# Rotating images by 180 degrees: all loads from one queue, the first group in four stepped transfers

## The chip, the cores and the metric

The kernel runs on one core of a Trainium2 chip. The metric is the device time of one execution in microseconds; of the kernel before, three runs took 122.02, 122.11 and 122.21, median 122.11.

## The reference

The input is 32 x 3 images of 256 x 256 float32 numbers. Each image is turned by 180 degrees:

```python
def reference(x: np.ndarray) -> np.ndarray:
    return np.rot90(x, k=2, axes=(-2, -1)).astype(np.float32)
```

Seen as a flat list of 65,536 numbers, an image is simply reversed. Nothing is computed; 25.17 MB are read, and 25.17 MB are written.

## The kernel before

The 96 images form three groups of 32 (G = 32, L37 to L40). Within a group, each image is cut into four sections of E = 16,384 numbers (64 KB). Partition p = 4n + s of a tile holds section s of image n, so a group fills 128 partitions of 64 KB each. Three such tiles, `A`, `Bt` and `Ct`, hold the three groups at the same time; a fourth, `T`, has room for J = 2048 numbers per partition and serves as scratch.

A group passes three steps. `load` (L54, L55) brings it in with one DMA of 128 rows. `turn` (L73) reverses every partition's 16,384 numbers in place: it calls `swap` (L61) for a strip of at most 2048 columns at the left and its mirror strip at the right, and each swap is three VectorE copies (all recorded at L52): right strip reversed to T, left strip reversed to the right, T to the left. `store` (L57, L58) writes the tile back; the order of the four sections within an image is reversed by the access pattern on the DRAM side (`[:, ::-1, ...]`), which walks 32 images of 4 sections.

The order of the work is written out by hand. The loads stand first (L69 to L71): A and Ct are issued by SyncE (SP), Bt by ScalarE (ACT), which does nothing else. The loads of A and Ct share SP's DMA queue with all the stores, and that queue serves transfers in the order of issue; Bt's load has ACT's queue for itself. VectorE's copies are kept in program order: three of A's four strips (`turn(A, 0, half - J)`, L80), a strip of 1008 columns of Bt (MID, L82), the last strip of A (L83), the rest of Bt (L85), all of Ct (L87). A's store is split: columns 0 to 255 (LEAD, L81), which are final after the first swap, and the other 16,128 columns (L84). The stores of Bt and Ct (L86, L88) are whole. SP issues a store when VectorE has finished the strips that it holds.

Of the kernel before, what the change touches and what calls it, by code (L numbers as in the profile page):

```python
# [2 lines left out]

os.environ.setdefault("NEURON_RT_ULTRASERVER_MODE", "4")

# [4 lines left out]


@with_exitstack
def kernel(
    ctx: ExitStack,
    tc: tile.TileContext,
    x: bass.AP,
    out: bass.AP,
):

    nc = tc.nc
    P = 128

    B, C, H, W = x.shape
    L = H * W
    G = 32
    E = L // 4
    J = E // 8

    x4 = x.rearrange("b c h w -> (b c) (h w)").rearrange(  # L37
        "(g n) (s e) -> g (n s) e", n=G, s=4)
    o4 = out.rearrange("b c h w -> (b c) (h w)").rearrange(
        "(g n) (s e) -> g n s e", n=G, s=4)  # L40

    pool = ctx.enter_context(tc.tile_pool(name="slots", bufs=1))
    A = pool.tile([P, E], x.dtype, tag="A")
    Bt = pool.tile([P, E], x.dtype, tag="B")
    Ct = pool.tile([P, E], x.dtype, tag="C")
    T = pool.tile([P, J], x.dtype, tag="T")

    def back(t, lo, hi):
        return t[:, hi - 1:(lo - 1 if lo else None):-1]

    def copy(dst, src):
        tc.keep_in_program_order(nc.vector.tensor_copy(out=dst, in_=src))  # L52

    def load(t, g, lo, hi, queue=nc.sync):  # L54
        return queue.dma_start(out=t[:, lo:hi], in_=x4[g][:, lo:hi])  # L55

    def store(t, g, lo, hi):  # L57
        return nc.sync.dma_start(  # L58
            out=o4[g][:, ::-1, lo:hi], in_=t[:, lo:hi])

    def swap(t, lo, w):  # L61
        hi = E - lo - w
        copy(T[:, 0:w], back(t, hi, hi + w))
        copy(t[:, hi:hi + w], back(t, lo, lo + w))
        copy(t[:, lo:lo + w], T[:, 0:w])

    MID = 1008
    LEAD = 256
    load(A, 0, 0, E)  # L69
    load(Bt, 1, 0, E, nc.scalar)  # L70
    load(Ct, 2, 0, E)  # L71

    def turn(t, lo, hi):  # L73
        while lo < hi:
            w = min(J, hi - lo)
            swap(t, lo, w)
            lo += w

    half = E // 2
    turn(A, 0, half - J)  # L80
    store(A, 0, 0, LEAD)  # L81
    turn(Bt, 0, MID)  # L82
    turn(A, half - J, half)  # L83
    store(A, 0, LEAD, E)  # L84
    turn(Bt, MID, half)  # L85
    store(Bt, 1, 0, E)  # L86
    turn(Ct, 0, half)  # L87
    store(Ct, 2, 0, E)  # L88


# [1 line left out]
_INS = ['x']  # L92
_OUTS = [((32, 3, 256, 256), 'float32')]


# [23 lines left out]
```

## Time and profile before

| what | value |
|---|---|
| median of three runs | 122.11 us |
| span of the profiled execution, first to last instruction | 120.5 us (its time outside the span isn't listed; the median is 1.6 us above the span) |
| VectorE busy | 44.7 us, 39 copies; one of 128 x 2048 takes 1.23 us |
| load of A (SP) and of Bt (ACT), issued at 0.73, to landing | 41.2 and 41.4 us |
| load of Ct (SP), issued at 1.18, to landing | 60.5 us |
| first copy of VectorE | at 41.99 us |
| stores issued to landing: A small, A large, Bt, Ct | 16.3, 21.9, 27.6, 31.8 us |
| DMA traffic | 50.33 MB, mean 418 GB/s over the span |

A DMA is shared out over the core's 16 DMA engines. The trace records each packet of each engine; here a packet is one row of one partition (64 KB, or 1 KB in A's small store), and every transfer ends on each engine with a packet of 4 bytes that raises a semaphore. "Issue" is the instruction on SP or ACT that hands the transfer over; "landing" is the moment when its last semaphore update has arrived. Queue 1 is SP's, queue 10 is ACT's.

The profile's stretches give for each window the busy time of the engines, the granted clock, the mean busy share of the DMA engines and the bytes moved. The list of waits says who waited for whom, and how long.

### The profile page before, as it was taken

To read this page: it belongs to the slowest core of one execution; us is meant where nothing else is said; L and a number is where in the kernel's file an instruction comes from. 1 tells how busy PE (TensorE), PEld (TensorE's weight loads), DVE (VectorE), ACT (ScalarE), POOL (GpSimd) and SP (SyncE) were. 2 spreads that over 40 slices of the span, in tenths; PEclk is the share of its full clock that TensorE was granted. 3 is DMA by queue.
4 is the path that set the end of the run, shared out by engine and by line. 5 is a ranking of instruction groups with operands and counts; after the bars stand their busy time and mean duration, and the time that the engine had idled before them with its cause. 6 is when DMAs were issued, how large, how long until landed. Compare 5 with 4: busy or idle time off the path is not lost.

```text
span 120.5 us, 96 instructions
## 1 busy us (share of the span) xinstructions
DVE 44.7 (37%) x39; POOL 0.2 (0%) x4
## 2 busy tenths in 40 slices
DVE  0000000000000099999999999999910000000000
POOL 0000000000000000000000000000000000000000
DMA  9888988898889888988999977988898889888980
GB/s 348 348 348 370 674 348 348 370 652 370 348 370 652 370 348 348 674 370 348 348 386 599 428 343 343 664 369 348 348 674 370 348 348 674 370 348 348 674 370 0
DMA packets 1008, 50.33 MB, mean 418 GB/s; under 512 B 112, under 2 KB 240, under 8 KB 240
## 3 DMA queue, kind: packets, MB, share of 16 engines
q1 hardware_dynamic: 864, 41.94, 81.3%
q10 hardware_dynamic: 144, 8.39, 16.1%
HBM read 25.17 MB, written 25.17 MB: 418 GB/s over the span
## 4 chain that ended last, share of the span: by engine, by line
DVE 37%; DMA 34%; issue 1%
DMA A<-in_x_dram 34%; DVE T L52 12%; DVE Bt L52 9%; DVE A L52 8%; DVE Ct L52 8%
## 5 line engine op out<-in xcount | busy, mean ns | idle before, releaser
L52 DVE COPY T<-A 128x2048 f32<-128x2048 f32 x4 | 4.9, 1227 | 42.1 <-DMA A<-in_x_dram 42.0
L52 DVE COPY Bt<-T 128x2048 f32<-128x2048 f32 (+2 forms) x5 | 5.1, 1014 | 0.2
L52 DVE COPY T<-Bt 128x2048 f32<-128x2048 f32 (+2 forms) x5 | 5.1, 1014 | 0.2
L52 DVE COPY Bt<-Bt 128x2048 f32<-128x2048 f32 (+2 forms) x5 | 5.1, 1013 | 0.2
L52 DVE COPY T<-Ct 128x2048 f32<-128x2048 f32 x4 | 4.9, 1228 | 0.1
L52 DVE COPY A<-T 128x2048 f32<-128x2048 f32 x4 | 4.9, 1227 | 0.1
L52 DVE COPY Ct<-T 128x2048 f32<-128x2048 f32 x4 | 4.9, 1227 | 0.1
L52 DVE COPY Ct<-Ct 128x2048 f32<-128x2048 f32 x4 | 4.9, 1227 | 0.1
L52 DVE COPY A<-A 128x2048 f32<-128x2048 f32 x4 | 4.9, 1226 | 0.1
L103 POOL MEMSET const-bfloat16-1.0<- 128x1 bf16 x1 | 0.1, 101 | 0.0
L103 POOL MEMSET const-uint8-127<- 128x1 uint8 x1 | 0.1, 101 | 0.0
L103 POOL MEMSET const-float32-0.0<- 128x1 f32 x1 | 0.1, 98 | 0.2 <-issue 0.2
L103 POOL MEMSET const-float32-1.0<- 128x1 f32 x1 | 0.1, 98 | 0.0
## 6 DMA issues: line engine op xcount, KB each, us to landing
out_dram<-A SPq DMA_DIRECT2D x1, 8064.0 KB, 21.9
out_dram<-A SPq DMA_DIRECT2D x1, 128.0 KB, 16.3
Bt<-in_x_dram ACTq DMA_DIRECT2D x1, 41.4
A<-in_x_dram SPq DMA_DIRECT2D x1, 41.2
Ct<-in_x_dram SPq DMA_DIRECT2D x1, 60.5
out_dram<-Bt SPq DMA_DIRECT2D x1, 27.6
out_dram<-Ct SPq DMA_DIRECT2D x1, 31.8
```

The costliest lines, as they stand in the source:

```text
L52: tc.keep_in_program_order(nc.vector.tensor_copy(out=dst, in_=src))
L103: nc = _bacc.Bacc("TRN2", target_bir_lowering=False, num_devices=1)
```

## The change

ScalarE no longer issues a load. SyncE issues all of them: group 0 in four transfers of 32 rows, where transfer j brings section j of all 32 images to the partitions j, j + 4, j + 8, ...; then group 1 whole, then group 2 whole. The copies, the stores and their order stay. (Eight empty lines are also taken out, so that line numbers after the change are lower by 8 up to the loads.)

```diff
     MID = 1008
     LEAD = 256
-    load(A, 0, 0, E)
-    load(Bt, 1, 0, E, nc.scalar)
+    for j in range(4):
+        nc.sync.dma_start(out=A[j::4, :], in_=x4[0][j::4, :])
+    load(Bt, 1, 0, E)
     load(Ct, 2, 0, E)
```

VectorE's first copy of A then waits for four semaphores in place of one, and so does A's small store. In the order of instructions, ACT loses its one DMA; SP has ten DMAs in place of six.

## The prediction

> **What bounds the kernel now.** I first read the page's top lines: VectorE, the only engine that computes, is busy 37% of the span, so it can't be the bound by itself. Then the lines of the DMA queues, and the busy time by stretches, cut where one transfer ends and the next begins (columns: stretch and its length, busy time of DVE and POOL, clock, mean busy share of the 16 DMA engines, GB/s):
>
> ```profile
> span 120.5 us, 96 instructions
> ...
> DVE 44.7 (37%) x39; POOL 0.2 (0%) x4
> ...
> q1 hardware_dynamic: 864, 41.94, 81.3%
> q10 hardware_dynamic: 144, 8.39, 16.1%
> ```
>
> ```profile
> ...
> 1.75:41.60 39.84, 0.00 (x0) 0.00 (x0) 1.00 1.04 446
> 41.60:61.20 19.60, 18.66 (x17) 0.00 (x0) 1.00 0.91 385
> 61.20:80.20 19.00, 18.45 (x17) 0.00 (x0) 1.00 1.00 434
> 80.20:99.50 19.30, 7.54 (x7) 0.00 (x0) 1.00 1.00 435
> 99.50:118.80 19.30, 0.00 (x0) 0.00 (x0) 1.00 1.00 435
> ```
>
> The two queues fill 81.3 + 16.1 = 97.4% of 16 engines' span. The transfers follow each other without a hole: A with Bt to 41.6, Ct to 61.2, then the stores of A, Bt, Ct at 434 to 435 GB/s. (A packet is booked at its end, which makes the first share 1.04 and the second 0.91.) The trace's packet records say how. A packet is one row of 64 KB; each engine moves 8 rows of each group. The first row takes 2.70 to 3.37 us (median 3.10), every other load row up to 44 us 2.418 to 2.44, every 64 KB store row 2.418, one beginning each 2.4145. Each engine has 48 such rows in a chain: 48 x 2.4145 = 115.9, the pieces of A's store counted as 8 whole rows. Beside them stand 0.7 for the first row, about 0.4 in the last Ct rows, 1.76 before the first packet and about 1.1 after the last, and the staggering of the engines. That is the 120.5.
>
> The list of waits names something else:
>
> ```profile
> DVE T L52 <- DMA A<-in_x_dram: 42.0, 1, 42.0
> ```
>
> VectorE stands still for 42.0 us until A has landed. The reader is to see that this wait is long and yet not the bound: the engines work all through it. The page's DMA issues (line, queue, count, KB, us from issue to landing) show the same for the stores:
>
> ```profile
> out_dram<-A SPq DMA_DIRECT2D x1, 8064.0 KB, 21.9
> out_dram<-A SPq DMA_DIRECT2D x1, 128.0 KB, 16.3
> ...
> out_dram<-Bt SPq DMA_DIRECT2D x1, 27.6
> out_dram<-Ct SPq DMA_DIRECT2D x1, 31.8
> ```
>
> 128 KB take 16.3 us to land because they stand behind Ct's load in SP's queue: issued at 45.77, their packets move at 60.93 and after. Ct's store, issued at 88.0, lands at 119.7: it needs 19.3 and waits 11 behind Bt's. The queue is served in the order of issue.
>
> **The change, part by part.**
>
> *A comes first, alone.* Before, A and Bt take turns row by row (queue 1, queue 10), so both land at 42. After, A's 8 rows per engine run first: the slowest engine ends its first row at 5.38, seven more make 5.38 + 7 x 2.4145 = 22.3, and with the 0.5 from the last packet to the landing (41.61 to 42.14 now) VectorE starts at about 22.8 in place of 41.99. Nine copies of A at a pitch of 1.26 end at 34.1. The next copies read Bt, which lands at 42 as before (the bytes ahead of it are the same), so VectorE stops for 8 us. Then 3 x 0.72 on Bt and 3 x 1.26 on A: the large store of A goes out at about 48.0 (59.3 now). Bt's remaining 13.6 end at 61.6 (72.8 now); Ct has landed at 61.7, its 15.1 end at 76.9 (88.0 now).
>
> *What that is worth: nothing.* The stores stand behind the loads in the queue and begin at 61 in either kernel. A's large store is needed there at about 61.3; its first packet would come 1.0 after issue (0.73 to 1.76 at the start), so it is 12 us early, where it is 1 early now. Bt's is needed at 80.2, Ct's at 99.5; both are ready long before, now too (72.8 and 88.0). The 19 us on VectorE and the 11 us on the issues become waiting in the queue. The stall that goes was never the late one; the queue is.
>
> *Bt moved from ACT's queue to SP's.* ACT issues nothing else and is released from its 0.38 of issue. On SP, Bt's issue moves behind four of A's and Ct's behind five, at 0.45 a piece (0.73 to 1.18 now): Bt at 2.5, Ct at 3.0. Engines have A's rows until 21, so neither is missed. Nothing else waits on SP: its next instruction is A's small store.
>
> *A in four transfers.* Three more issues and, per engine, three more 4-byte semaphore packets of 9 ns on the path: +0.03. The second quarter is issued at 1.2 and has packets at about 2.2; an engine asks for it after two rows, at about 7.2, so the cover is 5 us. Were the cover gone, an engine would idle by what is missing. Does the border of two transfers itself cost? In one queue the large store of A is followed by Bt's, Bt's by Ct's: the records show a 9 ns packet and the next row at once. Loads behind loads: A's end (41.0) to Ct's first row, the same, though queue 10 ended there too. I take 0; the upper end is a restart like the very first row's, 0.64 (the mean of the 16 first rows, 3.06, less 2.418) at each of four borders: 2.6.
>
> *The first row.* First packets leave from 1.755 to 2.483 over the engines, first rows end from 4.75 to 5.38. A first transfer with a quarter of the rows and no second issuer beside it may start the late engines sooner. If all ended as the earliest: -0.63. If the latest start met the longest excess (0.95): 2.48 + 2.42 + 0.95 = 5.85, +0.47. The late starters had the short excess (0.28 to 0.41), so start and end are loosely tied, and I take -0.1.
>
> *A store waiting longer in the queue.* Ct's rows are even until A's small store is issued at 45.8; the five rows that follow it show medians 5, 0, 27, 7, 26 ns over 2.418 (sum 0.07), and the last load row 0.35. If the queued store is the cause, the five become twelve rows (issued at 26.6): 12 x 0.013 = 0.16, +0.09; at 27 each +0.26. If not, 0 (or -0.07 were they to vanish). I take +0.05. The 0.35 belongs to the last load row ahead of the stores, which stays.
>
> *The end.* SP's last waits get three more semaphores, all long fired: 0.02 each, +0.05. VectorE's first copy and A's small store wait for four instead of one: off the path.
>
> Sum against the span: -0.1 + 0.03 + 0.05 + 0.05 = +0.03, so 120.5 again. The median of the runs, 122.11, is 1.6 above that span; the page doesn't split it, and nothing in the change touches it. 122.1.
>
> **A rule that speaks against it.** The Trainium skill (SBUF — State Buffer, "Can I just issue two DMAs to hit both halves?") says that only one transfer spanning all 128 partitions reaches all 16 ports, and its section on the setup-cost knee puts about 2 us of fixed cost on each transfer; three more would give 122.1 + 6 = 128 as an estimate by that page. The rows here show no such cost between queued transfers (9 ns), so the measured border is used. By the port map of the same page (Door 1), every fourth partition meets each port twice, so the first half of the rule need not bite if the rows are dealt to the engines by port; that dealing no row of before shows for 32 rows.
>
> **The rivals.**
>
> *Slower: the 32 rows are dealt unevenly.* All of the above needs two rows of each quarter on each engine, with no two engines in each other's way. If only 8 engines carry them (or two share one way into SBUF), A takes 16 row times instead of 8 on those: +8 x 2.4145 = 19.3, 141.4. It decides as soon as an engine gets three rows of each quarter (+9.7). Against it: the stores' DRAM side is walked as 32 x 4 rows (issue forms 32x4x16384), and they run at 2.418 a row on all 16. For it: no 32-row load with stepped partitions is in the trace.
>
> *Slower: borders cost.* Each of the four new borders on the single queue costs some part of a restart, because loads behind loads on one queue alone were never seen: +0.3 to +2.6, say 123.4. Against: the store borders.
>
> *Faster: the start shrinks and the slowest engine with it.* The end is set by the slowest engine (last packets end from 118.85 to 119.40), and its lag dates from the first row. At -0.4 for the start, 121.7; with a quiet queue as well 121.4. For it: the spread of 0.73 between engines at the start, with two issuers.
>
> **How the numbers follow.** About 0.2% (0.24 us) is what a measurement of this kernel can tell from no change. Forecast, within that: 0.44. Faster by the start: 0.28. Borders: 0.15. Uneven dealing: 0.13. So slower 0.28 in all. The range runs from 121.4 (the whole faster case but its end) to 123.4 (more than half of the borders): 0.44 + 0.27 + 0.09 = 0.80. The forecast's own range is 121.9 to 122.35.
>
> **What would show it.** Right: A's last quarter lands at about 22.5 and VectorE's first copy starts there, stops 8 us for Bt, the large store of A issues near 48, and yet Ct's store lands near 119.7. Queue 1 alone holds all 50 MB. Wrong: A landing at about 40 (uneven dealing); rows longer than 2.42 at the start of each quarter (borders); first rows all ending by 4.9 (the faster case); stores moving before 61 would overturn the order of the queue.

## The result and the profile after

The changed kernel is slower by about 1%: 123.25 us (median of 4 runs, 123.23 to 123.37) against 122.06 (4 runs, 121.82 to 122.21). The ratio over all runs is 1.0105, 95% interval 1.0091 to 1.0119 (the two medians alone give 1.0097). The profiled execution has a span of 121.6 us against 120.5.

The page of the changed kernel, lines that answer to those shown of before (its DMA issues: line, queue, count, KB, us from issue to landing):

```profile
span 121.6 us, 102 instructions
...
DVE 44.6 (37%) x39; POOL 0.2 (0%) x4
...
q1 hardware_dynamic: 1056, 50.33, 97.0%
...
out_dram<-A SPq DMA_DIRECT2D x1, 8064.0 KB, 33.8
out_dram<-A SPq DMA_DIRECT2D x1, 128.0 KB, 36.2
...
Ct<-in_x_dram SPq DMA_DIRECT2D x1, 58.8
out_dram<-Bt SPq DMA_DIRECT2D x1, 39.5
out_dram<-Ct SPq DMA_DIRECT2D x1, 42.8
```

One queue now holds all 50.33 MB, and the stores spend 11 to 20 us more between issue and landing: they wait in the queue. The list of waits of the changed kernel (who waited for whom, us, times, longest):

```profile
DVE T L44 <- DMA A<-in_x_dram: 23.1, 1, 23.1
DVE T L44 <- DMA Bt<-in_x_dram: 8.0, 1, 8.0
DVE T L44 <- DMA Ct<-in_x_dram: 0.9, 1, 0.9
```

VectorE starts at 23.1 instead of 42.0 and stops 8.0 for Bt, as worked out. The third line is new and small, and it is the trace of the loss: Ct lands at 62.7 (issued at 3.89, 58.8 to landing), 1.0 later than the 61.7 of before.

Where is that microsecond? Here are SP's and ACT's first issues in the timelines (start, duration, queue, line, what), of the changed kernel and then of before:

```profile
0.73 2.49 SPq L62 DMA_DIRECT2D A<-in_x_dram  x4
3.26 0.58 SPq L47 DMA_DIRECT2D Bt<-in_x_dram  x1
3.89 0.45 SPq L47 DMA_DIRECT2D Ct<-in_x_dram  x1
```

```profile
0.73 0.38 ACTq L55 DMA_DIRECT2D Bt<-in_x_dram  x1
0.73 0.39 SPq L55 DMA_DIRECT2D A<-in_x_dram  x1
1.18 0.43 SPq L55 DMA_DIRECT2D Ct<-in_x_dram  x1
```

A stepped quarter takes some 0.6 to issue (2.49 for four), a whole group 0.4 before; Bt's whole load right behind the quarters takes 0.58 as well. In the packet records the first packet leaves at 2.09 instead of 1.76, and the slowest engine ends its first row at 5.69 instead of 5.38: **+0.31**. This place varies from execution to execution: in the runs below that begin on a whole load (e1, e2, e4 to e7, e10, e11) the slowest first row ended at 5.25 to 5.57, in the other one that begins on a stepped quarter (e8) at 6.07. From there on the rows of A and Bt are 2.418 to 2.44 in both, also at the borders of the quarters.

The second place is the last row that each engine loads. The next two answers are the stretches around its end (stretch, length, busy DVE and POOL, clock, DMA share, GB/s; a packet is booked at its end, so a stretch in which no row ends shows 0). First the changed kernel, then before:

```profile
58.90:60.30 1.40, 1.36 (x2) 0.00 (x0) 1.00 0.00 0
60.30:61.50 1.20, 1.13 (x3) 0.00 (x0) 1.00 0.00 0
61.50:62.80 1.30, 0.40 (x2) 0.00 (x0) 1.00 2.13 895
```

```profile
58.90:60.30 1.40, 1.37 (x2) 0.00 (x0) 1.00 0.00 0
60.30:61.50 1.20, 1.17 (x2) 0.00 (x0) 1.00 1.78 744
61.50:62.80 1.30, 1.27 (x2) 0.00 (x0) 1.00 0.49 208
```

Before, the rows end in the middle stretch; after, in the last one. On the slowest engines the row before it ends at 58.60 and 58.84 (after), the last load row at 61.40 and 62.38: the lag grows there from 0.24 to 0.98, and 0.98 it stays until the last packet (119.40 and 120.38). (It had shrunk from 0.31 to 0.24 because five of Ct's rows were a little longer before, by 0.07 in sum.) A last load row takes 3.02 to 3.80 us, where an undisturbed one takes 2.42, and 2.73 to 2.80 in this profile of before. The end of the span adds 0.06.

### The profile page after: what moved, and what is told of

It reads as the page before. It is cut to its first block, busy times and chain, and to the rows that moved or that the text cites. A ratio compares the mean times of both kernels' runs of the same rounds, so it can differ in the third digit from the quotient of the medians.

```text
span 121.6 us, 102 instructions
## 1 busy us (share of the span) xinstructions
DVE 44.6 (37%) x39; POOL 0.2 (0%) x4
## 2 busy tenths in 40 slices
DMA packets 1056, 50.33 MB, mean 414 GB/s; under 512 B 160, under 2 KB 288, under 8 KB 288
## 3 DMA queue, kind: packets, MB, share of 16 engines
q1 hardware_dynamic: 1056, 50.33, 97.0%
## 4 chain that ended last, share of the span: by engine, by line
DMA 32%; DVE 28%; SPq 2%; issue 1%; another core or an unknown queue 1%; DVEq 0%
DMA Bt<-in_x_dram 32%; DVE T L44 9%; DVE Bt L44 8%; DVE Ct L44 8%; DVE A L44 2%; SPq L62 2%; DVEq L44 0%
## 5 line engine op out<-in xcount | busy, mean ns | idle before, releaser
L44 DVE COPY T<-A 128x2048 f32<-128x2048 f32 x4 | 4.9, 1227 | 23.2 <-DMA A<-in_x_dram 23.1
## 6 DMA issues: line engine op xcount, KB each, us to landing
Ct<-in_x_dram SPq DMA_DIRECT2D x1, 58.8
```

## The experiments

The theory after reading the two traces: A's stores, issued early because A lands early, stand in the queue behind the loads, and this lengthens the last load row (theory Q); the quarters cost only at the start. The rivals: the quarters do both, or the single queue does. "Row" below is the time of Ct's last load row over the 16 engines, from the packet records. Times are medians; the ratio is over all runs, to the kernel before on the same chip (its medians: 122.02 beside e1 to e4, 122.11 beside e5 to e8, 121.88 beside e9 to e11), and so not quite the quotient of the medians.

| run | edit | ratio (95%) | us | first packet | row, us |
|---|---|---|---|---|---|
| changed | quarters on SP, all loads on SP | 1.0105 (1.0091 to 1.0119) | 123.25 | 2.09 | 3.02 to 3.80 |
| e1 | three whole loads on SP | 1.0079 (1.0062 to 1.0096) | 123.13 | 1.74 | 2.95 to 3.77 |
| e2 | quarters on SP, Bt on ACT | 1.0008 (0.9995 to 1.0021) | 122.19 | 1.73 | 2.42 to 2.66 |
| e3 | blocks of 32 partitions, SP alone | 1.1705 (1.1684 to 1.1725) | 142.90 | 1.77 | 2.42 to 2.43 |
| e4 | e1, VectorE starts on Bt | 0.9996 (0.9984 to 1.0008) | 122.00 | 1.73 | 2.43 to 2.54 |
| e5 | e1, large store of A at 59.3 | 0.9994 (0.9984 to 1.0005) | 122.11 | 1.75 | 2.42 to 2.69 |
| e6 | e1, no small store | 1.0075 (1.0061 to 1.0090) | 123.05 | 1.74 | 3.29 to 3.97 |
| e7 | e1, large store of A at 55.4 | 1.0082 (1.0068 to 1.0096) | 123.27 | 1.74 | 3.21 to 3.86 |
| e8 | quarters, VectorE starts on Bt | 1.0034 (1.0016 to 1.0052) | 122.59 | 2.09 | 2.42 to 2.80 |
| e9 | e1, a crowded bit behind A | 1.0114 (1.0099 to 1.0129) | 123.36 | 1.75 | 2.42 to 2.43 |
| e10 | e1, stores on ACT | 1.0110 (1.0084 to 1.0136) | 123.25 | 1.73 | see below |
| e11 | before, once more | one run | 121.87 | 1.76 | 2.42 to 2.66 |

**e1: the quarters undone, all loads on SP.**

```diff
-    load(Bt, 1, 0, E, nc.scalar)
+    load(Bt, 1, 0, E)
```

> SP issues all three loads, each whole (A, Bt, Ct); the four quarters are undone. In the trace of the changed kernel two places are longer than before: the first row of A (first packets from 2.09 in place of 1.755, slowest first row ends at 5.69 in place of 5.38, +0.31) and the last load row of Ct (3.02 to 3.80 in place of 2.73 to 2.80). Theory Q (early stores): the last load row grows because A's stores are issued early and stand in the queue behind the loads, which comes from A landing early; the first row grows because of the quarters. Then here the first packet is back at about 1.76 and the last load row stays near 3.3: about 122.8. Rival S (the quarters do both): both go, 122.1. Rival R (the single queue does both): both stay, 123.2.

The first packet is back at 1.74, the row stays long. Most of the loss has nothing to do with the quarters: 0.79% of 122.0, 0.96 us (1.11 between the medians). The time is somewhat above theory Q's 122.8, since that sum took 3.3 for the row, and the slowest end moves by 3.64, from 58.70 to 62.34.

**e2: the quarters, with Bt back on ACT.**

```diff
-    load(A, 0, 0, E)
+    for j in range(4):
+        nc.sync.dma_start(out=A[j::4, :], in_=x4[0][j::4, :])
```

> A in four stepped quarters on SP, but Bt's load back on ACT. A and Bt alternate again, so A should land near 42 and the stores of A go out as late as before. Theory Q: first packet at 2.1, last load row back at 2.75: about 122.4. Rival S: both stay, 123.2. Rival R: both go, 122.1.

A's last quarter lands at 42.0 again, and the row is short. The first packet does not come late either, which I had expected for theory Q: the engines start on Bt's whole load from ACT, and A's late quarter is hidden behind it. No measurable change against before.

**e3: neighbouring partitions** (against e1).

```diff
-    load(A, 0, 0, E)
+    for j in range(4):
+        p = slice(32 * j, 32 * j + 32)
+        nc.sync.dma_start(out=A[p, :], in_=x4[0][p, :])
```

> SP issues all loads, A in four transfers of 32 neighbouring partitions instead of every fourth. If the dealing of rows to engines meets a limit by partitions, A's rows take longer than 2.42 and A lands well after 23 (up to 19 us later if two engines share a way), total up to 141. If not, the same 123.2 as the changed kernel, with the first packet at 2.1 if the number of transfers sets it and at 1.76 if the step does.

The stretches of this run, A's load, then those of Bt and Ct, then the stores:

```profile
5.40:41.60 36.20, 0.00 (x0) 0.00 (x0) 1.00 0.99 203
41.60:81.20 39.60, 28.69 (x26) 0.00 (x0) 1.00 0.99 424
81.20:139.90 58.70, 15.96 (x14) 0.00 (x0) 1.00 0.99 429
```

A's load moves 203 GB/s with all 16 engines busy: share 0.99, rows of 4.93 to 5.13 us (from the second on), over twice 2.418. So the engines are in each other's way by partition, and the step of four is what keeps the changed kernel's quarters at full speed. The Trainium skill (SBUF — State Buffer, "Door 1: The DMA port swizzle") says that partitions 0 to 31 reach 8 of 16 ports; the rate agrees with it, being about half of the 424 GB/s of the loads that follow. The first packet is at 1.77: the step, not the number of transfers, delays it to 2.09. And the last load row is 2.42 to 2.43 although A's stores were as early as in e1:

```profile
47.59 21.89 SPq L58 DMA_DIRECT2D out_dram<-A  x2
```

The large store's issue ends at 69.48, 9.3 us before that row begins (78.79), and in e1 it ends 9.2 us before (48.73, row at 57.96); the "12 us" of the expectation of e9 count to the row's end. That spoke against the plain form of theory Q and led to e9.

**e4: as e1, with the stores late** (against e1).

```diff
-    turn(A, 0, half - J)
+    turn(Bt, 0, MID)
+    turn(A, 0, half - J)
     store(A, 0, 0, LEAD)
-    turn(Bt, 0, MID)
     turn(A, half - J, half)
```

> As e1 (three whole loads on SP), but VectorE turns the first strip of Bt before it begins A, so that it starts at 42 and A's stores are issued as late as in the kernel before (small one near 48, large one near 59). Theory Q: last load row back at about 2.75, 122.1. Rival R (the single queue lengthens the last load row, whenever the stores are issued): last load row 3.3 as in e1, 122.8.

The loss is gone, on the same single queue with the same three loads. Only VectorE's order differs, and with it the issue of the stores (A's large one at 59.3 again). The rival of the single queue falls. In the stretches of e1 and then of e4 the rows' end moves from the last stretch to the middle one:

```profile
60.30:61.50 1.20, 1.17 (x2) 0.00 (x0) 1.00 0.06 20
61.50:62.80 1.30, 0.30 (x2) 0.00 (x0) 1.00 2.07 877
```

```profile
60.30:61.50 1.20, 1.17 (x2) 0.00 (x0) 1.00 2.31 969
61.50:62.80 1.30, 1.26 (x2) 0.00 (x0) 1.00 0.00 0
```

**e5, e6, e7: which store, and how early** (against e1). e5 and e7 move A's last strip behind three and two large strips of Bt (k = 3, 2); e6 stores A in one piece.

```diff
     store(A, 0, 0, LEAD)
     turn(Bt, 0, MID)
+    turn(Bt, MID, MID + k * J)
     turn(A, half - J, half)
     store(A, 0, LEAD, E)
-    turn(Bt, MID, half)
+    turn(Bt, MID + k * J, half)
```

e6:

```diff
-    store(A, 0, 0, LEAD)
...
-    store(A, 0, LEAD, E)
+    store(A, 0, 0, E)
```

> Three whole loads on SP as in e1, VectorE starts on A at 23 and the small store is issued at 26.6 as there, Bt's store near 61.6 as there. Only the last strip of A comes after three large strips of Bt, so the large store of A goes out at about 59.4 instead of 48.2. Theory Q1 (the large store, standing in the queue while the last load row moves, lengthens that row): last load row back to 2.42 to 2.80, about 122.1. Theory Q2 (the small store's early issue does it): row stays at 3.0 to 3.8, 123.1. Theory Q3 (Bt's store, issued at 61.7 at the turn, does it): stays, 123.1.

> As e1, but A is stored in one transfer of 64 KB rows, issued at 48.2; there is no small store. Q1: last load row stays long, about 123.1. Q2: it goes back to 2.42, about 121.9 (the small packets' own time is the same bytes). Q3: stays, 123.1.

> As e5, but A's last strip after two large strips of Bt: the large store is issued at about 55.6, some 2.5 us before the last load row begins, and VectorE copies Bt during that row as in e1. Q1 with a threshold (it is enough that it is queued before the last row starts): 3.0 to 3.8 as in e1, 123.1. Q1 with a dose (the longer it waits, the more): between, about 122.5. Q2 and Q3: 123.1.

SP's stores of A (both issues in one line, from the start of the small one to the end of the large one) and the middle stretch, in e5:

```profile
26.40 33.45 SPq L58 DMA_DIRECT2D out_dram<-A  x2
```

```profile
60.30:61.50 1.20, 1.15 (x2) 0.00 (x0) 1.00 2.18 916
```

and in e7:

```profile
26.34 29.67 SPq L58 DMA_DIRECT2D out_dram<-A  x2
```

```profile
60.30:61.50 1.20, 1.10 (x2) 0.00 (x0) 1.00 0.01 2
```

The large store's issue ends at 59.85 in e5, and the rows end on time; it ends at 56.01 in e7, and they don't. The last load row begins at 57.9 to 58.5 in both. So it is the large store, and a threshold rather than a dose: 2 us ahead of that row costs as much as 9 (e1, e6, e7). No run tells where the threshold lies between e7's issue, which ends 2 us before the row begins, and e5's, which starts at 59.3, about 1 us into it. The small store alone, early in e5, costs nothing measurable; without it (e6) the loss stays. Bt's store goes out at 61.5 in e5 too, without harm.

**e8: the quarters, with the stores late** (the changed loads with e4's order).

```diff
-    turn(A, 0, half - J)
+    turn(Bt, 0, MID)
+    turn(A, 0, half - J)
     store(A, 0, 0, LEAD)
-    turn(Bt, 0, MID)
     turn(A, half - J, half)
```

> The changed loads as they are (SP alone, A in four stepped quarters), but VectorE starts with Bt's first strip as in e4, so that both stores of A go out as late as in the kernel before. What stays is the cost of the quarters alone: first packet at 2.1, slowest first row 0.1 to 0.3 later. Theory Q (any form): last load row 2.42 to 2.80, 122.2 to 122.4. Rival (quarters share in the longer last row): 3.0 or more, 123.2.

1.0034, about 0.41 us (0.20 to 0.63), is what the stepped quarters cost by themselves. First packet at 2.09, slowest first row at 6.07 (in an execution of 123.03, one of the slowest of its twelve); the median is a little above the expected range. With e1's 0.96 the two make 1.37, against 1.28 for the change as a whole (1.0105 of 122); the intervals cover the difference.

**e9: reads ahead of writes?** (against e1)

```diff
-    load(A, 0, 0, E)
+    load(A, 0, 0, E - 1024)
+    for j in range(4):
+        p = slice(32 * j, 32 * j + 32)
+        nc.sync.dma_start(out=A[p, E - 1024:E], in_=x4[0][p, E - 1024:E])
```

> Why does the early large store not lengthen the last load row in e3 (2.43 there), though it stood in the queue 12 us before that row as in e1? Theory B: an engine reads ahead of what it writes; where the next packet is a store's, its reads delay the last load's data, and in e3 the crowded quarters had held the writes back, so that the reads were far ahead and the delay found data in store. Here A's last 1024 columns come in four blocks of 32 neighbouring partitions (crowded as in e3, but only 4 KB per row), the rest as in e1, stores early as in e1. The crowded bit costs about 8 rows of 4 KB at the double time, 1.2 us more. Theory B: last load row back to about 2.43, in total 123.1 + 1.2 - 0.9 = 123.4. Rival (something else in e3, for example its late start of A, spared the row): row stays at 3.0 to 3.8, in total 124.3.

Theory B's numbers came out: row 2.42 to 2.43, 123.36. The stores are as early as in e1 or the changed kernel relative to the row, as the timeline and the stretches of e9 show (the large one's issue ends at 49.97, 9.2 us before the last load row begins):

```profile
27.95 22.02 SPq L58 DMA_DIRECT2D out_dram<-A  x2
```

```profile
58.90:60.30 1.40, 1.36 (x2) 0.00 (x0) 1.00 1.73 749
60.30:61.50 1.20, 1.16 (x2) 0.00 (x0) 1.00 0.00 0
61.50:62.80 1.30, 1.24 (x2) 0.00 (x0) 1.00 2.13 895
```

Here the row before the last ends in the first stretch and the last one in the third, 2.42 later on each engine. The lag of this kernel lies at the crowded bit near 22 us: the first whole row behind it takes 2.59 to 2.97 us (2.64 to 3.27 in e3). Paid there, it isn't paid at the end. VectorE copies Bt during the last load row here as in e1, so its work isn't what lengthens that row.

**e10: the stores on ACT's queue** (against e1).

```diff
     def store(t, g, lo, hi):
-        return nc.sync.dma_start(
+        return nc.scalar.dma_start(
```

> As e1, but all stores are issued on ACT's queue, so that A's stores need not wait behind Ct's load: they alternate with Ct's last five rows. If every change from a load row to a store row costs what the last one costs in e1 (0.5 to 1.3), five more of them give about 126. If only the last costs, 123.1. If mixing hides the change, 122.0.

The loss is about that of e1, once (the two intervals overlap). ACT's stores of A, and the stretches around the long row:

```profile
26.45 22.33 ACTq L58 DMA_DIRECT2D out_dram<-A  x2
```

```profile
51.00:51.70 0.70, 0.70 (x1) 0.00 (x0) 1.00 5.06 1498
51.70:53.50 1.80, 1.73 (x3) 0.00 (x0) 1.00 0.00 0
53.50:54.30 0.80, 0.80 (x1) 0.00 (x0) 1.00 0.00 0
54.30:55.50 1.20, 1.17 (x2) 0.00 (x0) 1.00 1.98 860
```

No row ends from 51.7 to 54.3, which is longer than an undisturbed row takes. The load row that begins at 51.0 to 51.6, over 2 us after the large store's issue has ended (48.78), takes 3.12 to 3.95 us, while the one before it, which begins near that end (48.6 to 49.2), takes 2.418; after the long row, load rows of 2.418 in the median and store rows of 2.380 alternate without further loss. So here it is the first change from loads to a large store that costs, though another queue holds the store, and it is paid once. Of my three forecasts "only the last costs" gave the right time, though the place is the first change, not the last.

**e11: the kernel before again.**

> The kernel before once more, for a second profile: whether its last load row of Ct (2.73 to 2.80 in the first profile) is the same again or varies as in e2, e4 and e5 (2.42 to 2.69).

It varies: 2.42 to 2.66 here, 2.73 to 2.80 in the first profile. In the kernel before, the large store's issue (59.3) falls into the last load row, and the cost is between none and 0.38.

## Why the prediction was wrong

- **The bound and the queue: right.** The engines work without a hole in their chain of 48 rows; the stores stand behind the loads; VectorE's 19 us become waiting. A landed at 23.1 (22.8 forecast), the large store went out at 48.3 (48.0). The last landing, forecast near 119.7, came at 120.7.
- **"What that is worth: nothing": the step that failed.** I took a store that is 12 us early for as good as one that is 1 early, and wrote that the 0.35 of the last load row "stays". That term was mis-sized: it is 0 to 0.39 where the large store comes during that row (before, e2, e4, e5, e8) and 0.5 to 1.5 where it is queued 2 to 9 us before the row starts (changed, e1, e6, e7). By e1 this is worth 0.96 us (0.76 to 1.17). I had the row of 0.35 in hand, the only place where a load meets a store, and gave it neither a cause nor bounds.
- **The first row: wrong side.** Taken as -0.1 between -0.63 and +0.47; it was +0.31, and the quarters alone cost 0.41 (0.20 to 0.63) by e8, in whose profile the slowest first row ended at 6.07, beyond the 5.85 taken as the latest. I had charged a stepped quarter the 0.45 of a whole group; an issue takes about 0.6, and the first packet comes 0.35 later than a whole load's (e1).
- **Borders: right.** 2.418 at each, no restart. The rival's price, 123.4, lies near the result, but its mechanism did not occur.
- **A store waiting in the queue, +0.05: not there.** The five rows before the last have medians of 2.418 to 2.422 in the changed kernel, and 2.418 to 2.421 in the second profile of before; the 0.07 belonged to one execution.
- **The end, +0.05: right** (0.06). From the last packet to the end of the span it takes 1.18 to 1.20 us in the runs with the stepped quarters (changed, e2, e8) and 1.12 to 1.14 in those with three loads.
- **Uneven dealing: didn't happen.** The form that the prediction put in brackets, engines that share a way into SBUF, is what e3 fits with neighbouring partitions: all 16 engines carry rows, each row takes twice as long, +20.9 us against the 19.3 estimated.
- **The rule that spoke against it.** The Trainium skill's rule that only one transfer spanning all 128 partitions reaches all 16 ports (SBUF — State Buffer, "Can I just issue two DMAs to hit both halves?") fits e3 and not the stepped quarters, which ran at 2.418 a row. The fixed cost per transfer of about 2 us (the same page, "The DMA setup-cost knee") appeared at no border between the quarters.

What stays inferred is why the large store costs. Two things are shown: it costs when it is issued 2 us before the load row in front of it begins and not when it is issued about 1 us into that row (e7, e5), and the loss does not come behind loads of 32 neighbouring partitions (e3, e9). Theory B would explain both: the engine reads ahead, and the store's reads from SBUF delay the last reads from HBM unless those are far ahead. The Trainium skill (DMA: Bandwidth & Descriptors, "Two DMAs through the same engine are not ordered") states that an engine's read and write sides are separate queues; the records here show whole packets, not the two sides, so no run shows the mechanism itself. Nor do the runs tell it from a rival: that such a loss comes once, wherever the rows are first disturbed, since in e3 and e9 the first whole row behind the crowded loads was long, and in e10 only the first turn was.

No version here beats the kernel before: e4 and e5 equal it.

## What to carry to other kernels

Where the DMA engines are full from end to end, as here, work that is ready sooner can be worth nothing and can even cost (0.96 us by e1): look at every place where loads turn to stores, and ask what will be queued there that wasn't before. A row of the profile that differs from its neighbours (0.35 us on the last load row) is a price whose condition is unknown; give it bounds or test it before calling it constant. When a change frees an engine that isn't the bound, an order that keeps the later issues where they were (e4, e5) tells at once whether the earliness itself does harm.

## What the runs showed of the hardware

- A load of 32 neighbouring partitions ran at half speed with all engines busy (203 GB/s, rows of about 5.1 us); 32 partitions at a step of four ran at full speed (2.418).
- A stepped load's issue took about 0.6 us, as did the whole load's issue right behind four of them (0.58 to 0.60), and its first packet left at 2.09; a block of 32 neighbours or a whole group elsewhere took 0.4 to 0.5, first packet at 1.73 to 1.77.
- A large store issued 2 us or more before the last load row ahead of it lengthened that row by 0.5 to 1.5 us (changed, e1, e6, e7), and from another queue it lengthened the first load row that began over 2 us after its issue, by 0.7 to 1.5 us (e10); rows of loads and stores that alternated afterwards lost nothing.
- Behind loads of 32 neighbouring partitions the same turn cost nothing (rows of 2.42 to 2.43 in e3 and e9).
